# Three seams of a three-layer kernel: only TensorE keeps the written order, output blocks run in pairs, residual transfers move to SP's queue

## The chip, the cores and the metric

The kernel runs on one core of one Trainium2 chip. The metric is the device time of one execution in microseconds. Before the change the median of three runs is 1291.76 us (1290.72 to 1292.23). The engines are named as the profile names them: PE is TensorE, DVE is VectorE, ACT is ScalarE, POOL is GpSimd and SP is SyncE, which here only issues DMAs.

## The reference

Three layers run one after the other on 512 tokens of width 1024, in float32:

```python
for i in range(2):                       # first_block
    h = rms_norm(x, pre_norm[i])
    y = gla_mixer(h, ...) if i == 0 else nsa_mixer(h, ...)   # both end in  o @ w_out
    x = x + rms_norm(y, post_norm[i])
# second_block, one hybrid layer
h = rms_norm(x, norm_gain) * (1 + scale) + shift             # scale, shift, gate from c
proj = h @ w_in
attn = stick_breaking_attention(q, k, v)
p_a = (attn * silu(z_a)) @ w_branch_a
p_b = (multiscale_causal_pool(u) * silu(z_b)) @ w_branch_b
out = (sigmoid(m_a) * p_a + sigmoid(m_b) * p_b) @ w_out
return rms_norm(x + gate * out, final_gain)
```

What matters here are the three places where one layer ends and the next begins: an output product of 512x1024 by 1024x1024, a norm of its rows, the addition to the residual, a second norm, and then the first product of the next layer. The last of them ends the kernel.

## The kernel before

Every float32 product is made of three matmuls on rounded high and low parts (`w_hi` with `hH`, `w_lo` with `hH`, `w_hi` with `hL`). A weight comes in units of 256 columns (280 for `w_tok`). `load_unit` fetches a unit in two halves of 512 KB into `w_raw`, which has two buffers, over SP's queue (L146); ACT rounds each half to `w_hi` (L149), DVE subtracts to get `w_lo` (L150), and only then is the raw buffer free for the half that comes next. ORDER is a list of the units in the order in which they are fetched ahead.

A **seam** is the stretch around one output product. There are three: GLA's output into the NSA layer (about 205 to 325 us), NSA's output into the stick-breaking (SB) layer (about 625 to 750 us), and the last one (from about 1233 us to the end). In each, `out_products` works through eight blocks (b, n): b is one of four groups of 128 tokens, n is one half of the 1024 output columns. A block is 48 matmuls of 256 columns, 24 for each of its two weight units, so a block with n = 0 needs units 0 and 1, and a block with n = 1 needs units 2 and 3. PSUM tiles for even b have the name `ps_pj`, those for odd b `ps_sc`.

At the first two seams `boundary` follows a block up. `each` copies the product to `x` on ACT (L463) and sums its squares (L384). When both halves of a group b are there, the generator `norm` is put in a list of chains with a due step. It computes the root on DVE (`rms`, ten small operations), multiplies and adds the residual `xr` (L424, L425), sums squares again on ACT, stores the new residual stream to `x1d` or `x2d` by DMA, pauses 4 steps, computes `rms` and the scaled copy `xs` (L432), pauses 4 steps, and then lets PE transpose `xs` (L438), ACT scale the transposes into `ntmp` (L443 or L445) and round them to `hH` (L448), and DVE make `hL` (L449). The first products of the next layer read `hH` and `hL`: groups 0 and 1 first, then 2 and 3. A step is one `tick`, which `proj_toks` calls every 12 matmuls of an output block.

What sets the order: between `in_order` and its end, the order of PE, DVE, ACT and POOL is the order in which the program emits the instructions, so each engine works through that list and waits in it. The rounding of a weight half is not emitted at once there: it goes to a list `splits` with a due step (`late`, else `lag`), and `run_splits` emits one per tick. SP is not in that set; its instructions are put in order by a scheduler. The residual reads (`reload`) and the stores of the residual stream are issued from POOL. The pool `wout` holds units 2 and 3 of the output weight; at the third seam it also holds the 2 MB residual `x2`, which is one DMA on SP's queue ahead of the loads of units 2 and 3.

Of the kernel before, what the change touches and what calls it, by code (L numbers as in the profile page):

```python
# [75 lines left out]
def tile_kernel(ctx, tc, xT, xR, post_r0, post_r1, fgain_r, pos, vecs, w_gla, w_glr, w_gk, w_gla_out, w_nsa, w_tok, w_nsa_out, b_gate,  # L76
                pe_k, pe_v, ck1, cv1, ck2, cv2, cvec, w_ada, w_in2, pool_w, w_ba, w_bb, w_o2, out, dbg=None):
    nc = tc.nc
    V, S, G, TE = nc.vector, nc.scalar, nc.gpsimd, nc.tensor
# [6 lines left out]
    def f32(ap):  # L86
        return ap.bitcast(F32)
# [46 lines left out]
    splits = None  # L134
# [33 lines left out]
    def tick():  # L168

        nonlocal step  # L170
        step += 1
        for ch in chains[:]:
            while ch[0] <= step:
                d = next(ch[1], None)
                if d is None:
                    chains.remove(ch)
                    break
                ch[0] = step + d
        run_splits()

    @contextmanager
    def in_order():

        nonlocal splits
        E = mybir.EngineType
        with tc.manual_schedule(engines={E.PE, E.DVE, E.Activation, E.Pool}):
            splits = []
            yield
            while chains:
                tick()  # L190
            while splits:
                splits.pop(0)[2]()
        splits = None
# [34 lines left out]
    def psum(tag):  # L228
        return ps.tile([P, 512], F32, tag=tag, name="ps_" + tag, bufs=BANKS[tag])
# [47 lines left out]
    def proj_toks(jobs, aH, aL, need=None):  # L277

        for k in range(KC):
            if need:  # L280
                if k % max(1, 4 // len(jobs)) == 0:
                    tick()
                    ensure(*(u for u, _, _, _ in jobs))
                need(jobs[0][1] * P, k)
            for (wh, wl), tb, p, n in jobs:
                s = slice(tb * P, tb * P + P)
                TE.matmul(p[:, :n], aH[:, k, s], wh[:, k, :n], start=(k == 0), stop=False)  # L287
                TE.matmul(p[:, :n], aH[:, k, s], wl[:, k, :n], start=False, stop=False)  # L288
                TE.matmul(p[:, :n], aL[:, k, s], wh[:, k, :n], start=False, stop=(k == KC - 1))  # L289
# [81 lines left out]
    xt = x.rearrange("p c t -> p (c t)").rearrange("p (b d) -> p b d", b=NB)  # L371

    def half(n):
        return slice(n * 512, n * 512 + 512)

    def rms(ss):

        v = npl.tile([P, 1], F32, tag="rsv1", name="rsv", bufs=2)
        V.scalar_tensor_tensor(v, ss[:, 0:1], EPS, ss[:, 1:2], op0=ALU.add, op1=ALU.add)
        return rsqrt(v, 1)  # L380

    def square_sum(src, ss, n):
        scr = npl.tile([P, 512], F32, tag="scr", name="scr", bufs=1)
        S.activation(scr, src, AF.Square, scale=1.0 / 32, accum_out=ss[:, n:n + 1])  # L384
# [6 lines left out]

    def reload(src, b, n):
        r = npl.tile([P, 512], F32, tag="xr", name="xr", bufs=3)
        G.dma_start(r, src[:, b, half(n)])
        return r

    def split_x():
# [3 lines left out]

    def out_products(us, each, freed=lambda: None):

        for b, n in ((0, 0), (1, 0), (2, 0), (0, 1), (1, 1), (3, 0), (2, 1), (3, 1)):
            p = psum("sc" if b % 2 else "pj")
            for i in range(2):
                proj_toks([(us[2 * n + i], b, p[:, 256 * i:256 * i + 256], 256)], hH, hL, lambda t0, k: None)
            each(b, n, p)
            if (b, n) == (3, 0):
                freed()  # L410

    def boundary(wsrc, gain, xsrc, keep, scale, shift, then, early, fp):

        norms_, chunks = {}, [0] * NB

        def norm(b, ss, xo):
            y = rms(ss)  # L420
            ss2 = npl.tile([P, 2], F32, tag="ss2", name="ss2", bufs=2)
            for n in range(2):
                xn_ = xt[:, b, half(n)]
                V.scalar_tensor_tensor(xn_, xn_, y, grow[:, half(n)], op0=ALU.mult, op1=ALU.mult)  # L424
                V.tensor_add(xn_, xn_, xo[n])  # L425
                square_sum(xn_, ss2, n)
            G.dma_start(keep[:, b], xt[:, b])
            yield 4
            y = rms(ss2)
            xs = [npl.tile([P, 512], F32, tag="xs", name="xs", bufs=2) for n in range(2)]  # L430
            for n in range(2):
                S.activation(xs[n], xt[:, b, half(n)], AF.Copy, scale=y)  # L432
            yield 4
            ts = slice(b * P, b * P + P)
            for n in range(2):
                pt = psum("tr")
                for i in range(4):
                    TE.transpose(pt[:, i * P:(i + 1) * P], xs[n][:, i * P:(i + 1) * P], ident)  # L438
                tmp = npl.tile([P, 4, P], F32, tag="ntmp", name="ntmp", bufs=2)
                for i in range(4):  # L440
                    c = 4 * n + i
                    if shift is None:
                        S.activation(tmp[:, i], pt[:, i * P:(i + 1) * P], AF.Copy, scale=scale[:, c:c + 1])  # L443
                    else:
                        S.activation(tmp[:, i], pt[:, i * P:(i + 1) * P], AF.Identity, scale=scale[:, c:c + 1],  # L445
                                     bias=shift[:, c:c + 1])
                cs = slice(4 * n, 4 * n + 4)
                S.copy(hH[:, cs, ts], tmp)  # L448
                V.tensor_sub(hL[:, cs, ts], tmp, f32(hH[:, cs, ts]))  # L449
                chunks[b] += 4  # L450
                yield 1

        def need(t0, k):
            for b in (t0 // 256 * 2, t0 // 256 * 2 + 1):
                while chunks[b] <= k:
                    next(norms_[b][1])

        SS, nus = {}, []

        def each(b, n, p):  # L460
            if n == 0:
                SS[b] = npl.tile([P, 2], F32, tag="ss", name="ss", bufs=4)
            S.copy(xt[:, b, half(n)], p)  # L463
            square_sum(p, SS[b], n)
            if n:
                norms_[b] = [step + 2, norm(b, SS[b], [reload(xsrc, b, n_) for n_ in range(2)])]
                chains.append(norms_[b])
                if b == 2:
                    nus.append(unit(*then[0]))

        with tc.tile_pool(name="wout", bufs=2) as pool:
            us = [unit(wsrc, u) for u in range(2)]
            us += [load_unit(wsrc, u, pool=pool, late=4 * u - 3) for u in (2, 3)]
            grow = row_of(gain)
            firsts = [load_unit(*u, pool=fp, late=13 + 4 * i) for i, u in enumerate(early)]
            out_products(us, each, go_on)
            nus.append(unit(*then[1]))
        return nus, firsts, need
# [81 lines left out]
    with tc.tile_pool(name="gla", bufs=1) as gp:  # L560
# [24 lines left out]
        keep = gp.tile([P, 8, 64], F32, name="keep")  # L585
# [217 lines left out]
    prefetch(2)  # L803
    split_x()
    first = ExitStack()
    first.enter_context(in_order())
    o = VEC["pre1"][0]
    fps = ExitStack()
    uts, ucs, need = boundary(w_gla_out, post_r0, xR, x1d, vec[:, o:o + 8], None, ((w_tok, 0), (w_tok, 1)),
# [311 lines left out]
    nc.sync.dma_start(gated.rearrange("c p -> p c"), mod[:, 16:24])  # L1121
    prefetch(2)
    split_x()
    first.enter_context(in_order())
    uvs, (uq, uk), need = boundary(w_nsa_out, post_r1, x1d, x2d, amul, mod[:, 0:8], ((w_in2, 8), (w_in2, 9)),
                                   ((w_in2, 0), (w_in2, 4)),
                                   fps.enter_context(tc.tile_pool(name="sb_first", bufs=2, side="right")))
# [3 lines left out]
    with tc.tile_pool(name="sb_qk", bufs=1) as qp, tc.tile_pool(name="sb_v", bufs=2) as vp, ExitStack() as later:  # L1131
# [182 lines left out]
        while chains:  # L1314
            tick()
        norms.close()
        u_first = between.enter_context(tc.tile_pool(name="u_first", bufs=1, side="right"))
        gp = later.enter_context(tc.tile_pool(name="sb", bufs=1))

# [127 lines left out]
    lag = 5  # L1447
    prefetch(2)
    split_x()
    with in_order(), tc.tile_pool(name="wout", bufs=2) as pool:  # L1450
        us = [unit(w_o2, u) for u in range(2)] + [load_unit(w_o2, u, pool=pool, late=4 * u - 3) for u in (2, 3)]
        x2 = pool.tile([P, NB, D], F32, name="x2", bufs=1)
        nc.sync.dma_start(x2, x2d)
        gate, fgain = row_of(gated.rearrange("c p -> (c p)")), row_of(fgain_r, "fgain")
        SS = {}

        def last(b):
            y = rms(SS[b])
            for n in range(2):
                xn_ = xt[:, b, half(n)]  # L1460
                V.scalar_tensor_tensor(xn_, xn_, y, fgain[:, half(n)], op0=ALU.mult, op1=ALU.mult)
                nc.sync.dma_start(out[:, b, half(n)], xn_)
            yield 0

        def each(b, n, p):
            if n == 0:
                SS[b] = npl.tile([P, 2], F32, tag="ss", name="ss", bufs=4)
            xn_ = xt[:, b, half(n)]
            V.tensor_mul(xn_, p, gate[:, half(n)])
            V.tensor_add(xn_, xn_, x2[:, b, half(n)])  # L1470
            square_sum(xn_, SS[b], n)
            if n:
                chains.append([step + 1, last(b)])

        out_products(us, each)
# [85 lines left out]
```

## Time and profile before

| | us |
|---|---|
| median of the runs (lowest, highest) | 1291.76 (1290.72, 1292.23) |
| the profiled execution | 1293.02 |
| its span | 1291.3 |
| PE busy in it | 1204.9 (93%) |
| mean granted clock of PE, share of full speed | 0.972 |

The profiled execution took 1.3 us more than the median and 1.7 us more than its own span. A wait of PE in the lists below is the idle time of PE ahead of an instruction and names the instruction of another engine that ended it. The granted clock is given as a share of 2.4 GHz; the chip's records of this kernel have two levels, 1.2 and 2.4 GHz, so a mean clock c over a stretch of L us says that 2(1-c)L us of it were at 1.2 GHz.

### The profile page before, as it was taken

How to read it: one execution, taken by the hardware profiler on the slowest of the kernel's cores; microseconds unless marked ns; L12 is line 12 of the kernel's file. 1: busy time of each engine (PE TensorE's matmuls, PEld its weight loads, DVE VectorE, ACT ScalarE, POOL GpSimd, SP SyncE). 2: the span in 40 equal slices, each digit the busy share in tenths (PEclk: the TensorE clock that was granted, in tenths of full speed). 3: DMA queues.
4: the chain of work that ended last, by engine and by line, in shares of the span. 5: the costliest groups of instructions: out<-in, count | busy, mean ns of one | idle time of the engine just before them, and what ended most of it. 6: DMA issues, size and time to landing. Idle time of an engine off the chain costs nothing.

```text
span 1291.3 us, 18606 instructions
## 1 busy us (share of the span) xinstructions
PE 1204.9 (93%) x6880; PEld 1021.9 (79%) x6880; DVE 809.6 (63%) x1534; ACT 627.4 (49%) x1308; POOL 292.2 (23%) x422
## 2 busy tenths in 40 slices
PE   6998999879989999999986999999999999999996
PEld 6788778879867777777886977889887878888886
DVE  7668886562569888776556258778857552223445
ACT  6542136551537767678555456766644332222321
POOL 2113121010002433323001046555613410000000
PEclk9999999889989999999988989999999999999998
DMA  6244734432442011111443022212124233322241
GB/s 200 66 163 160 237 90 155 139 119 84 140 125 60 13 50 33 46 37 33 131 131 115 1 66 66 65 56 77 65 75 146 74 98 98 95 88 93 93 155 66
DMA packets 38843, 122.76 MB, mean 95 GB/s; under 512 B 6352, under 2 KB 8528, under 8 KB 38112
## 3 DMA queue, kind: packets, MB, share of 16 engines
q1 hardware_dynamic: 36320, 113.18, 27.6%
q0 software_dynamic: 2432, 8.39, 2.0%
q8 instruction: 54, 0.88, 0.3%
q14 instruction: 37, 0.30, 0.1%
HBM read 111.58 MB, written 6.30 MB: 91 GB/s over the span
## 4 chain that ended last, share of the span: by engine, by line
PE 59%; DVE 16%; ACT 11%; issue 6%; DMA 4%; POOL 4%; SPq 0%; ACTq 0%; DVEq 0%; POOLq 0%
PE ps_pj L236 6%; PE ps_pj L238 6%; PE ps_pj L237 6%; ACT w_hi L149 3%; DVE w_lo L150 3%; PE ps_tr L491 3%; PE ps_pv L1083 3%; PE ps_sc L237 3%; PE ps_sc L236 3%; PE ps_sc L238 3%; PE ps_pj L247 2%; PE ps_pj L245 2%; PE ps_pj L246 2%; POOL us L1377 2%; PE ps_sc L288 1%
## 5 line engine op out<-in xcount | busy, mean ns | idle before, releaser
L150 DVE TENSOR_TENSOR w_lo<-w_raw,w_hi 128x1024 fp32r<-128x1024 f32 (+1 forms) x154 | 190.4, 1247 | 132.2 <-ACT w_hi L149 127.6
L149 ACT CAST w_hi<-w_raw 128x1024 fp32r<-128x1024 f32 (+1 forms) x154 | 159.0, 1050 | 161.1 <-PE ps_sc L237 60.1
L236 PE MATMUL ps_pj<-hH,w_hi 128*128 128x512 f32 x512 | 207.3, 405 | 8.7 <-DVE rtm L844 4.6
L238 PE MATMUL ps_pj<-hH,w_lo 128*128 128x512 f32 x512 | 206.9, 404 | 0.0
L237 PE MATMUL ps_pj<-hL,w_hi 128*128 128x512 f32 x512 | 205.9, 402 | 0.0
L236 PEld LDWEIGHTS ps_pj<-hH,w_hi 128*128 128x128 f32 x512 | 97.3, 190 | 33.2 <-issue 6.7
L1071 POOL TENSOR_SCALAR PB<-PB,sm 128x128 f32<-128x128 f32 (+3 forms) x128 | 76.8, 622 | 181.8 <-DVE sm L1067 112.5
L238 PEld LDWEIGHTS ps_pj<-hH,w_lo 128*128 128x128 f32 x512 | 97.3, 190 | 20.7 <-issue 0.5
L237 PEld LDWEIGHTS ps_pj<-hL,w_hi 128*128 128x128 f32 x512 | 97.1, 190 | 19.8 <-issue 0.2
L495 ACT CAST PTh<-ps_tr 128x512 fp32r<-128x512 f32 (+3 forms) x160 | 74.3, 481 | 68.7 <-PE ps_tr L491 64.5
L496 DVE TENSOR_TENSOR PTl<-ps_tr,PTh 128x512 fp32r<-128x512 f32 (+3 forms) x160 | 85.7, 550 | 33.6 <-ACT PTh L495 32.3
L287 PE MATMUL ps_pj<-w_hi,hH 128*128 128x256 f32 (+1 forms) x288 | 85.9, 299 | 14.1 <-ACT w_hi L577 8.3
L287 PE MATMUL ps_sc<-w_hi,hH 128*128 128x256 f32 (+1 forms) x320 | 92.9, 291 | 1.8 <-ACT w_hi L149 1.8
L288 PE MATMUL ps_sc<-w_lo,hH 128*128 128x256 f32 (+1 forms) x320 | 92.3, 289 | 0.6 <-DVE w_lo L150 0.6
L289 PE MATMUL ps_sc<-w_hi,hL 128*128 128x256 f32 (+1 forms) x320 | 91.8, 288 | 0.0
L289 PE MATMUL ps_pj<-w_hi,hL 128*128 128x256 f32 (+1 forms) x288 | 84.4, 294 | 4.3 <-DVE hL L357 4.3
L288 PE MATMUL ps_pj<-w_lo,hH 128*128 128x256 f32 (+1 forms) x288 | 84.7, 294 | 1.1 <-POOL w_lo L578 0.7
L245 PE MATMUL ps_pj<-hH,w_hi 128*128 128x512 f32 x176 | 72.7, 413 | 3.0 <-ACT w_hi L149 3.0
L1064 ACT ACTIVATE PB<-ps_sc,nmx 128x128 f32<-128x128 f32 (+3 forms) x128 | 66.7, 534 | 14.6 <-DVE nmx L1061 7.1
L247 PE MATMUL ps_pj<-hH,w_lo 128*128 128x512 f32 x176 | 70.8, 402 | 0.1
L246 PE MATMUL ps_pj<-hL,w_hi 128*128 128x512 f32 x176 | 70.7, 402 | 0.0
L287 PEld LDWEIGHTS ps_pj<-w_hi,hH 128*128 128x128 f32 x288 | 56.9, 198 | 15.0 <-ACT w_hi L577 8.3
(365 smaller groups left out, 2935.3 us busy)
## 6 DMA issues: line engine op xcount, KB each, us to landing
w_raw<-in_w_in_dram SPq DMA_DIRECT2D x64, 512.0 KB, 3.3
wada<-in_w_ada_dram SPq DMA_DIRECT2D x24, 512.0 KB, 4.3
w_raw<-in_w_nsa_dram SPq DMA_DIRECT2D x24, 512.0 KB, 3.7
w_raw<-in_w_gla_dram SPq DMA_DIRECT2D x22, 512.0 KB, 4.4
w_raw<-in_w_gla_out_dram SPq DMA_DIRECT2D x8, 512.0 KB, 4.1
w_raw<-in_w_nsa_out_dram SPq DMA_DIRECT2D x8, 512.0 KB, 3.3
w_raw<-in_w_bb_dram SPq DMA_DIRECT2D x8, 512.0 KB, 3.6
w_raw<-in_w_ba_dram SPq DMA_DIRECT2D x8, 512.0 KB, 4.2
```

What stands on the lines that cost most here:

```text
L149: S.copy(hi[:, :, s], raw)
L150: lo_on[j].tensor_sub(lo[:, :, s], raw, f32(hi[:, :, s]))
L236: TE.matmul(p[:m, :tn], wh[:, k, s], aH[:, k, ts], start=(k == 0), stop=False)
L237: TE.matmul(p[:m, :tn], wh[:, k, s], aL[:, k, ts], start=False, stop=False)
L238: TE.matmul(p[:m, :tn], wl[:, k, s], aH[:, k, ts], start=False, stop=(k == KC - 1))
L245: TE.matmul(p, wh[:, k, s], aH[:, k], start=(k == 0), stop=False)
L246: TE.matmul(p, wh[:, k, s], aL[:, k], start=False, stop=False)
L247: TE.matmul(p, wl[:, k, s], aH[:, k], start=False, stop=(k == KC - 1))
L287: TE.matmul(p[:, :n], aH[:, k, s], wh[:, k, :n], start=(k == 0), stop=False)
L288: TE.matmul(p[:, :n], aH[:, k, s], wl[:, k, :n], start=False, stop=False)
L289: TE.matmul(p[:, :n], aL[:, k, s], wh[:, k, :n], start=False, stop=(k == KC - 1))
L496: V.tensor_sub(pl[:, :m], pt[:, :m], f32(ph[:, :m]))
```

## The change

Five things change, at the seams only.

1. `in_order(True)` keeps the written order for PE alone. `splits` is then None, so the rounding of a weight half is emitted where the load is, and the scheduler puts ACT, DVE, POOL and SP in order by its own estimate. It holds through the SB layer's first products too, where a `first.close()` and a new `in_order()` bring the old regime back.
2. The blocks run in the order (0,0) (1,0) (0,1) (1,1) (2,0) (3,0) (2,1) (3,1) instead of (0,0) (1,0) (2,0) (0,1) (1,1) (3,0) (2,1) (3,1). `out_products` serves all three seams.
3. The two pauses in `norm` are 5 steps instead of 4.
4. `reload` and the stores of `x1d` and `x2d` are issued from SP instead of POOL: 8 reads of 256 KB and 4 writes of 512 KB at each of the first two seams.
5. The pool `wout` of `boundary` is opened with `reuse_waits="tile"`; that of the third seam is not.

```diff
-    def in_order():
+    def in_order(alone=False):
...
-        with tc.manual_schedule(engines={E.PE, E.DVE, E.Activation, E.Pool}):
-            splits = []
+        with tc.manual_schedule(engines={E.PE} if alone else {E.PE, E.DVE, E.Activation, E.Pool}):
+            splits = None if alone else []
...
-        G.dma_start(r, src[:, b, half(n)])
+        nc.sync.dma_start(r, src[:, b, half(n)])
...
-        for b, n in ((0, 0), (1, 0), (2, 0), (0, 1), (1, 1), (3, 0), (2, 1), (3, 1)):
+        for b, n in ((0, 0), (1, 0), (0, 1), (1, 1), (2, 0), (3, 0), (2, 1), (3, 1)):
...
-            G.dma_start(keep[:, b], xt[:, b])
-            yield 4
+            nc.sync.dma_start(keep[:, b], xt[:, b])
+            yield 5
...
-            yield 4
+            yield 5
...
-        with tc.tile_pool(name="wout", bufs=2) as pool:
+        with tc.tile_pool(name="wout", bufs=2, reuse_waits="tile") as pool:
...
-    first.enter_context(in_order())          # first and second seam
+    first.enter_context(in_order(True))
...
+        first.close()                        # after the SB layer's first products
+        first.enter_context(in_order())
...
-    with in_order(), tc.tile_pool(name="wout", bufs=2) as pool:      # third seam
+    with in_order(True), tc.tile_pool(name="wout", bufs=2) as pool:
```

On ACT at the first seam, before: in the written order the squares of group 2 (`scr` from `x`) and a rounding of `w_tok` stand between the two `hH` of group 1.

```order
L443 ACTIVATE ntmp<-ps_tr,vec 128x128 x4
L448 CAST hH<-ntmp 128x4x128
L384 ACTIVATE scr,ss_2566<-x 128x512 x2
L149 CAST w_hi<-w_raw 128x8x140
L443 ACTIVATE ntmp<-ps_tr,vec 128x128 x4
L448 CAST hH<-ntmp 128x4x128
```

The same place on ACT now.

```order
L443 ACTIVATE ntmp<-ps_tr,vec 128x128 x4
L149 CAST w_hi<-w_raw 128x8x140
L448 CAST hH<-ntmp 128x4x128
L463 COPY x<-ps_pj 128x512
L384 ACTIVATE scr,ss<-ps_pj 128x512
L443 ACTIVATE ntmp<-ps_tr,vec 128x128 x4
L448 CAST hH<-ntmp 128x4x128
```

The squares taken from `x`, which wait for DVE's chain of the other group, have left the place between the two `hH`; a copy of a product block and its squares stand there instead.

On SP at the second seam, before: the loads of the output weight and of the gain row, then the weights of the next layer, with nothing between.

```order
L146 DMA w_raw<-in_w_nsa_out_dram 128x1024 x5
L389 DMA grow<-in_post_r_dram 128x1024
L146 DMA w_raw<-in_w_nsa_out_dram 128x1024 x3
L146 DMA w_raw<-in_w_in_dram 128x1024 x39
```

The same place on SP now; `xr` are the residual reads, `x2d` the stores.

```order
L389 DMA grow<-in_post_r_dram 128x1024
L146 DMA w_raw<-in_w_nsa_out_dram 128x1024
L394 DMA xr<-x1d 128x512 x2
L146 DMA w_raw<-in_w_nsa_out_dram 128x1024
L394 DMA xr<-x1d 128x512
L146 DMA w_raw<-in_w_nsa_out_dram 128x1024
L146 DMA w_raw<-in_w_in_dram 128x1024 x5
L394 DMA xr<-x1d 128x512
L146 DMA w_raw<-in_w_in_dram 128x1024
L427 DMA x2d<-x 128x1024
L394 DMA xr<-x1d 128x512 x2
```

The residual reads of group 0 now stand ahead of the two halves of unit 3, and the second read of group 1 behind five halves of the next layer's weights.

On ACT where the SB layer's first products end, before: the rounding of the next unit (`w_hi`) comes behind a table load and two activations of the first attention slot.

```order
L1148 CAST SV<-ps_sc 128x4x64 x2
L1245 ACT_TABLE_LOAD
L1245 ACTIVATE be<-ps_sc 128x256
L1246 ACTIVATE sg<-ps_sc 128x256
L149 CAST w_hi<-w_raw 128x8x128 x2
```

The same place now.

```order
L149 CAST w_hi<-w_raw 128x8x128 x2
L1148 CAST SV<-ps_sc 128x4x64 x2
L1245 ACT_TABLE_LOAD
L1245 ACTIVATE be<-ps_sc 128x256
L1246 ACTIVATE sg<-ps_sc 128x256
```

The two roundings have moved ahead of the last copies of `SV`.

## Rows read from the trace of the kernel before

**Rows 1.** The page, its span and part 1 (busy, share, instructions).

```profile
span 1291.3 us, 18606 instructions
...
PE 1204.9 (93%) x6880; PEld 1021.9 (79%) x6880; DVE 809.6 (63%) x1534; ACT 627.4 (49%) x1308; POOL 292.2 (23%) x422
```

**Rows 2.** Waits of PE, 200 to 340 us: total, times, longest.

```profile
PE ps_tr L438 <- ACT xs L432: 7.5, 3, 3.1
PE ps_pj L273 <- ACT hH L448: 5.3, 1, 5.3
...
PE ps_pj L236 <- ACT w_hi L149: 1.6, 2, 1.4
```

**Rows 3.** Waits of PE, 620 to 800 us.

```profile
PE ps_tr L438 <- ACT xs L432: 8.8, 3, 4.5
PE ps_pj L273 <- ACT hH L448: 5.5, 1, 5.5
PE ps_pj L245 <- ACT w_hi L149: 3.0, 1, 3.0
PE ps_pj L287 <- DVE SQs L1170: 2.7, 2, 1.6
```

**Rows 4.** Stretches: length, busy of PE, PEld, DVE, ACT, POOL, clock, DMA, GB/s.

```profile
200.00:340.00 140.00, 122.01 (x929) 117.91 (x928) 73.45 (x168) 69.27 (x144) 11.25 (x21) 0.95 0.42 134
620.00:760.00 140.00, 118.39 (x854) 113.69 (x855) 67.93 (x161) 72.83 (x155) 14.31 (x29) 0.89 0.30 98
...
1240.00:1244.00 4.00, 4.00 (x36) 4.00 (x35) 0.71 (x2) 0.00 (x0) 0.00 (x0) 1.00 0.97 401
```

**Rows 5.** ACT's timeline, first seam: start, duration, instruction, idle before it.

```profile
222.70 0.59 ACT L463 COPY x<-ps_pj 128x512 f32<-128x512 f32 x1 [0.36 <-PE ps_pj L289]
...
228.39 0.59 ACT L463 COPY x<-ps_pj 128x512 f32<-128x512 f32 x1 [0.32 <-PE ps_pj L289]
...
236.07 0.64 ACT L384 ACTIVATE scr<-x 128x512 f32<-128x512 f32 x1 [4.72 <-DVE x L425]
...
242.27 1.33 ACT L432 ACTIVATE xs<-x,rsy 128x512 f32<-128x512 f32 x2 [2.08 <-DVE rsy L307]
```

**Rows 6.** DVE's timeline in the same stretch.

```profile
231.38 1.23 DVE L150 TENSOR_TENSOR w_lo<-w_raw,w_hi 128x1024 fp32r<-128x1024 f32 x1 [2.05 <-ACT w_hi L149]
232.52 0.15 DVE L379 SCALAR_TENSOR_TENSOR rsv<-ss 128x1 f32<-128x1 f32 x1
...
234.49 0.75 DVE L424 SCALAR_TENSOR_TENSOR x<-x,rsy,grow 128x512 f32<-128x512 f32 x1
```

**Rows 7.** ACT's timeline ahead of the longest wait of that seam.

```profile
264.11 0.63 ACT L384 ACTIVATE scr<-x 128x512 f32<-128x512 f32 x1 [4.13 <-DVE x L425]
...
266.18 1.11 ACT L149 CAST w_hi<-w_raw 128x1120 fp32r<-128x1120 f32 x1
267.20 1.13 ACT L443 ACTIVATE ntmp<-ps_tr,vec 128x128 f32<-128x128 f32 x4
```

**Rows 8.** ACT's timeline where the SB layer's first products end.

```profile
746.18 1.28 ACT L1245 ACT_TABLE_LOAD   x1
...
748.01 1.99 ACT L149 CAST w_hi<-w_raw 128x1024 fp32r<-128x1024 f32 x2
```

**Rows 9.** ACT's timeline, second seam: last half of unit 3, then the third block.

```profile
639.35 1.05 ACT L149 CAST w_hi<-w_raw 128x1024 fp32r<-128x1024 f32 x1 [1.52 <-DMA w_raw<-in_w_nsa_out_dram]
641.41 0.59 ACT L463 COPY x<-ps_pj 128x512 f32<-128x512 f32 x1 [1.01 <-PE ps_pj L289]
```

**Rows 10.** PE's timeline, third seam, middle of block (0,1).

```profile
1255.66 0.39 PE L288 MATMUL ps_pj<-w_lo,hH 128*128 128x256 f32 x1 [0.38 <-DVE w_lo L150]
```

**Rows 11.** DMA issues, 624 to 660 us: count, KB each, median us to landing.

```profile
w_raw<-in_w_nsa_out_dram SPq DMA_DIRECT2D x4, 512.0 KB, 3.6
xr<-x1d POOLq DMA_DIRECT2D x4, 256.0 KB, 5.7
```

**Rows 12.** What SP's queue waited for, 200 to 340 us.

```profile
SPq L146 <- DVE w_lo L150: 43.9, 14, 8.4
```

More of the change, by code (lines that the diff above doesn't have):

```diff
@@ L1123, in tile_kernel @@
     split_x()
-    first.enter_context(in_order())
+    first.enter_context(in_order(True))
     uvs, (uq, uk), need = boundary(w_nsa_out, post_r1, x1d, x2d, amul, mod[:, 0:8], ((w_in2, 8), (w_in2, 9)),
```

## The prediction

> **What bounds the kernel now.** I read the page first: PE is busy 1204.9 of 1291.3 us [rows 1], so nothing but idle PE or a slow PE can be won back, 86 us in all. Then the list of PE's waits, cut to the first two seams. At the first, PE waits 7.5 us in three pieces for the scaled copies `xs` of the norm, 5.3 us in one piece for `hH` and 1.6 us for a rounded weight: 14.4 us [rows 2]. At the second it waits 8.8 and 5.5 us for the same two, 3.0 us for a weight that ACT rounds late and 2.7 us for `SQs`: 20.0 us [rows 3]. Then the table of stretches: over 140 us around each seam the mean granted clock is 0.95 and 0.89 [rows 4], so 2 x 0.05 x 140 = 14 us and 2 x 0.11 x 140 = 31 us ran at 1.2 GHz instead of 2.4. Those stretches follow the waits; PE loses half of them, less the part in which it is idle anyway. Last, the timelines of ACT and DVE, to see why the norm is late.
>
> There, group 0 of the first seam is the pattern. Its last block is copied at 228.39 us; blocks are 228.39 - 222.70 = 5.69 us apart, which is 48 matmuls at 0.119 us [rows 5]. The copy and its squares need about 1.3 us, so the norm could begin near 229.7. DVE begins it at 232.52, right behind a weight split of 1.23 us that was emitted ahead of it [rows 6]. The two squares of the residual stream follow at 236.07, after ACT had idled 4.72 us, and the `xs` start at 242.27; the first is ready after half of 1.33 us [rows 5], 14.6 us after the copy began. About 3 us of the 14.6 are the late start; the chain itself takes 11 to 12. The longest wait has another cause: ACT stands 4.13 us at the squares of a later group, whose input DVE has not made, then rounds a half of `w_tok` for 1.11 us, and only then scales the transposes of group 1, at 267.20 [rows 7]. PE needed them before that.
>
> **The change, part by part.** *Blocks in pairs, longer pauses.* In PE's written order 108 matmuls stood between the end of group 0's last block and its transposes, 12.8 us. Now (1,1), (2,0) and 36 matmuls of (3,0) stand there, 132 or 15.6 us, which covers the 14.6 even if nothing in the chain becomes faster. I count 132 to 140 matmuls for the other groups too. Between the second half of group 1's transposes and the first product that reads them stand 48 matmuls or 5.7 us, where there were 24 or 2.9.
>
> *Order on ACT, DVE and POOL.* The squares that blocked ACT for 4.13 us no longer stand between the two `hH` of group 1. The scheduler puts what it expects to be ready first, so a wrong expectation can cost what the written order cost; a rounding of `w_tok` still stands there, 1.11 us. I leave 3.5 of the first seam's 14.4 us (bounds 0 and 14.4): the last two groups have little between their transposes and their first use, 12 to 36 matmuls or 1.4 to 4.3 us, beside about 1.13 us for four scaled copies and as much again for `hH` and `hL`. That is **-10.9**. Where the SB layer's first products end, the table load of 1.28 us and two activations held the next unit's roundings until 748.01 [rows 8]; these now stand ahead, so the wait of 3.0 goes. Of the second seam's 20.0 us I leave 5 (bounds 0 and 20), more than at the first because a residual read now stands behind five weight halves there: **-15.0**.
>
> *Weights one block earlier.* Block (0,1) is the first to need units 2 and 3, and it moves from fourth to third place: 5.7 us earlier, while nothing in the third seam makes its loads earlier. The order of SP and ACT is the same there and its `wout` pool is untouched. Before, the second half of (0,1) started when DVE's last `w_lo` of unit 3 was done, at 1255.66, with a wait of 0.38 [rows 10]: already on the edge. Now the same matmul starts at the same time by the clock of the loads, but with one whole block fewer done. The loss is that block: **+5.7** (bounds 3, if the scheduler's freedom on DVE pulls a split forward, and 6.5). Two waits of about 2 and 4 us bring a low clock with them: **+2.0** (0 to 4). At the second seam the last rounding of unit 3 starts at 639.35 and takes 1.05 us, its split 1.23 us [rows 6, 9], so it was done at 641.6. The third block is copied at 641.41, so (0,1) started there [rows 9]; now it starts at 635.7 and its second half wants unit 3 at 638.6. With unchanged loads PE waits 3.0 us. Up to 1.7 more come if the three residual reads now ahead of it in SP's queue cost their own transfer time; nothing if the first halves, rounded when they land and not at a due step, free `w_raw` 3 us sooner. I take **+2.0** (0 to 4.7). At the first seam the loads of unit 3 were early enough to move by a block, and I take 0.
>
> *The DMA queue.* POOL's 12 issues per seam go and SP gains them; both engines wait most of the time, so issuing costs nothing. A residual read of 256 KB took 5.7 us from POOL beside weight halves of 512 KB that took 3.6 from SP [rows 11]. On SP's queue reads and weights follow one another. Over the third seam's 2 MB load that queue alone moved 401 GB/s [rows 4], far above the 134 and 98 GB/s of the seams, so its rate does not bind; what can bind is its order. The Trainium skill, "DMA: Bandwidth & Descriptors", section "Issuing engines are not separate DMA queues", says that DMAs run on the same 16 engines and interleave whichever engine issues them, so a second issuer adds no bandwidth; the 401 GB/s from one queue agree. By that rule the move costs no bandwidth, and the sum would be the same.
>
> *Clock.* Of the 45 us at 1.2 GHz, PE was idle in part of them. If all 34.4 us of waits lay inside, (45 - 34.4) / 2 = 5 us are lost; if none, 22. Waits come before the low stretch and reach into it, so I take 16 us lost now. With 10.5 of 34.4 us of waits left, a third of it stays: **-11.0** (0 to -20).
>
> *Sum.* -10.9 - 15.0 + 5.7 + 2.0 + 2.0 - 11.0 = -27.2. The profiled execution took 1293.0 us, so 1265.8; the median of the runs lies 1.3 us below it, which gives **1264.5 us**, and I predict 1265. Its own range is 1256 to 1274.
>
> **The rivals.** *Half of the gain.* The waits shrink but do not go, and a short wait still brings a low clock: 17 us of waits stay instead of 10.5, the clock gives back 5 instead of 11: 6.5 + 6 us more, 1277.5. For it: the scheduler's order is an estimate, and 1.6 us of rounding waits lie in the first seam already. Against it: the extra 24 matmuls per group need no estimate.
>
> *All of it.* No wait of the norms is left, unit 3 is in time at the second seam, the clock stays up: 8.5 + 2 + 5 us less, 1249. For it: cover above the chain for all groups. Against it: the third seam's loss is in all cases.
>
> *Slower: one queue, one order.* SP issues in order and each weight half waits for a free raw buffer, up to 8.4 us at a time at this seam, 43.9 us in all [rows 12]. A residual read behind five such halves (at 3.6 us each, if they do not overlap, 18 us) reaches a norm that wants it within 2 to 3 us of its block, and a store that waits for a norm holds the weights behind it. If reads come more than the 1.0 us of slack (15.6 - 14.6) late for each group, the waits stay as long as they were, 34.4 us and their clock; the third seam's 7.7 and the second's 2.0 remain: 1291.8 + 9.7 = 1301. It decides from about 4 us of lateness per group, eight groups. Against it: halves overlap, with two buffers and a queue that was idle for much of the seam.
>
> *No net change.* The waits of the norms fall by no more than the new waits for weights and their clock bring, about 10 us: 1292.
>
> **How the numbers follow.** The forecast 0.48, half of the gain 0.23, all of it 0.13, slower 0.11, no net change 0.05. The range 1249 to 1289 takes in the first three and leaves out the last two and the far end of the third. This kernel's runs tell a change of about 0.2% or 2.6 us. Faster than that: 0.84; within it: 0.05; slower: 0.11.
>
> **What would show it.** In the profile after: the waits on `xs` and `hH` at both seams under 4 us each in total, and the mean clock of the two 140 us stretches above 0.96. The wait of 3.0 us on a rounded weight at the SB layer's start gone. A new pair of waits at the third seam on `w_hi` and `w_lo` of units 2 and 3, 5 to 7 us together, with the same landing times counted from the seam's start. At the second seam a wait of 0 to 5 us in front of (0,1). I am wrong if the `xs` waits stay because their residual read lands late (then SP's order decides), or if the third seam shows no new wait.

## The result and the profile after

The changed kernel takes 1245.73 us (median of 4 runs, 1245.01 to 1249.45) against 1291.99 for the kernel before (4 runs): a ratio of 0.9649, 95% interval 0.9628 to 0.967, or 46.3 us less. The forecast was 1265 with a range down to 1249; the time lies 3 us below the range, near the rival "all of it" (1249). The profiled execution took 1246.3 us, its span is 1244.6 us, its mean granted clock 0.989 where it was 0.972.

The page, span and part 1, against [rows 1]:

```profile
span 1244.6 us, 18577 instructions
...
PE 1188.1 (95%) x6880; PEld 1010.8 (81%) x6880; DVE 800.6 (64%) x1534; ACT 626.8 (50%) x1308; POOL 279.1 (22%) x398
```

PE's busy time fell by 16.8 us with the same 6880 matmuls: that is work done at the higher clock. The other 30 us of the 46.7 are idle time that went.

All waits of PE between 200 and 335 us (engine, line, what it waited for; total, times, longest), against [rows 2]:

```profile
PE ps_pj L289 <- DVE hL L357: 2.4, 1, 2.4
```

The three waits of before, 14.4 us together, are gone, and nothing took their place: the row that is left is a wait in the first output block, which was 2.4 us before too.

The waits of PE between 590 and 760 us that belong to the seam, against [rows 3]:

```profile
PE ps_tr L438 <- ACT xs L432: 2.1, 1, 2.1
...
PE ps_pj L288 <- DVE w_lo L150: 0.9, 1, 0.9
PE ps_pj L287 <- ACT hH L356: 0.8, 1, 0.8
PE ps_tr L438 <- ACT ntmp L445: 0.6, 1, 0.6
```

Of 20.0 us, 2.1 are left; 0.6 on `ntmp` and 0.9 in the middle of block (0,1) came new. The wait of 3.0 us for a weight at the SB layer's start and that on `SQs` are gone.

The stretches around the first two seams and the start of the third, columns as in [rows 4]:

```profile
200.00:340.00 140.00, 137.49 (x1091) 131.84 (x1090) 78.17 (x190) 74.55 (x165) 6.71 (x12) 0.99 0.44 145
595.00:735.00 140.00, 133.87 (x978) 125.95 (x976) 82.24 (x185) 89.61 (x186) 24.58 (x38) 0.99 0.33 110
1180.00:1210.00 30.00, 24.47 (x170) 23.44 (x169) 13.40 (x19) 8.76 (x14) 0.00 (x0) 0.89 0.39 141
```

The clock of 0.95 and 0.89 became 0.99 and 0.99: of 45 us at 1.2 GHz some 6 are left. In the third seam 2 x 0.11 x 30 = 6.6 us at 1.2 GHz came new.

PE's timeline in the middle of block (0,1) of the third seam, against [rows 10]:

```profile
1201.58 0.38 PE L287 MATMUL ps_pj<-w_hi,hH 128*128 128x256 f32 x1 [0.85 <-ACT w_hi L149]
1202.84 0.39 PE L288 MATMUL ps_pj<-w_lo,hH 128*128 128x256 f32 x1 [0.88 <-DVE w_lo L150]
```

Counted from the seam's first wait on `hL` (1237.68 before, 1184.50 after), the matmul that needs unit 3's `w_lo` starts at 17.98 before and at 18.34 now. It waits for the same thing at nearly the same time, with one block fewer done.

Where the time went, by spans of the two traces. The marks are the starts of the first matmul after each seam's wait on `hL` L357, of the first L940 and of the first L1289 on `PTl`.

| stretch | before | after | difference |
|---|---|---|---|
| up to the first seam | 207.0 | 203.6 | -3.4 |
| first seam and NSA's first products | 122.4 | 102.0 | -20.4 |
| NSA layer | 297.4 | 295.8 | -1.6 |
| second seam and SB's first products | 150.0 | 123.4 | -26.6 |
| SB and pool branch | 461.0 | 459.7 | -1.3 |
| third seam to the end | 53.6 | 60.1 | +6.5 |

The first, third and fifth rows are stretches that the change leaves alone. Over the 15 profiles (the two kernels and the 13 versions below) the first takes 203.6 to 208.4 us, the third 295.8 to 297.9, the fifth 459.5 to 461.1. Stretches at 1.2 GHz come and go there in the same code; of the 6.3 us that the three rows add here, 5.7 are busy time of PE. In the eleven versions made from the changed kernel the three add up to 961.4 to 966.4 us, against 965.4 before and 959.1 here, so the 6.3 us are not counted to the change. The seams alone give 40.5 us.

### The profile page after: what moved, and what is told of

It is laid out like the page before. It is cut to its first block, busy times and chain, and to the rows that moved or that the text cites. A ratio compares the mean times of both kernels' runs of the same rounds, so it can differ in the third digit from the quotient of the medians.

```text
span 1244.6 us, 18577 instructions
## 1 busy us (share of the span) xinstructions
PE 1188.1 (95%) x6880; PEld 1010.8 (81%) x6880; DVE 800.6 (64%) x1534; ACT 626.8 (50%) x1308; POOL 279.1 (22%) x398
## 4 chain that ended last, share of the span: by engine, by line
PE 63%; DVE 13%; ACT 8%; issue 6%; DMA 5%; POOL 4%; SPq 0%; DVEq 0%; ACTq 0%; POOLq 0%
PE ps_pj L236 6%; PE ps_pj L238 6%; PE ps_pj L237 5%; DVE w_lo L150 3%; PE ps_tr L491 3%; PE ps_pv L1083 3%; PE ps_sc L237 3%; PE ps_sc L236 3%; PE ps_sc L238 3%; ACT w_hi L149 3%; PE ps_sc L288 2%; PE ps_sc L289 2%; PE ps_sc L287 2%; PE ps_pj L245 2%; PE ps_pj L247 2%
## 5 line engine op out<-in xcount | busy, mean ns | idle before, releaser
L149 ACT CAST w_hi<-w_raw 128x1024 fp32r<-128x1024 f32 (+1 forms) x154 | 159.0, 1052 | 169.4 <-PE ps_sc L237 60.4
L238 PEld LDWEIGHTS ps_pj<-hH,w_lo 128*128 128x128 f32 x512 | 96.6, 189 | 20.4 <-issue 0.2
L237 PEld LDWEIGHTS ps_pj<-hL,w_hi 128*128 128x128 f32 x512 | 96.7, 189 | 19.5 <-issue 0.2
L1064 ACT ACTIVATE PB<-ps_sc,nmx 128x128 f32<-128x128 f32 (+3 forms) x128 | 66.7, 534 | 14.4 <-DVE nmx L1061 7.1
```

The source lines that it names most:

```text
L149: S.copy(hi[:, :, s], raw)
L237: TE.matmul(p[:m, :tn], wh[:, k, s], aL[:, k, ts], start=False, stop=False)
L238: TE.matmul(p[:m, :tn], wl[:, k, s], aH[:, k, ts], start=False, stop=(k == KC - 1))
```

## The experiments

Times are medians, with the ratio to the kernel before and its interval. "Seams" gives the second, fourth and last rows of the table above for that kernel's profile.

**Old blocks in the third seam.**

```diff
-        out_products(us, each)
+        out_products(us, each, old=True)     # (0,0) (1,0) (2,0) (0,1) ... there alone
```

> The changed kernel, but the third seam alone works through its eight blocks in the old order. My theory: pairs cost the third seam one block, 5.7 us, and about 1 us of low clock, because units 2 and 3 cannot come earlier there; the trace shows the third seam 6.5 us longer than before. Then this runs at 1239 to 1240 us, the waits on w_hi and w_lo of that seam fall from 4.2 us to under 1 us. Rival: the third seam is longer because ACT and DVE are ordered by the scheduler there; then this stays at 1245 to 1246.

Measured 1242.79 us, 0.9623 (0.9605 to 0.9642); seams 101.9, 123.2, 52.1. The only wait over 0.2 us that is left in its third seam:

```profile
PE ps_pj L289 <- DVE hL L357: 1.4, 1, 1.4
```

The seam is 8.0 us shorter than with pairs, though the scheduler orders ACT and DVE there as well; the rival falls. The median gained 3 us, not the 6 expected, and its interval overlaps that of the changed kernel: its profile spent 2.4 and 2.0 us more ahead of the first seam and in the NSA layer, in code that is the same.

**Written order back at the first two seams.**

```diff
-    first.enter_context(in_order(True))
+    first.enter_context(in_order())
```

> The changed kernel with the written order of PE, DVE, ACT and POOL back at the first two seams (splits deferred again); pairs, pauses of 5, SP's queue and the third seam as changed. Theory A (the free order of ACT and DVE brings most, since late rounding and squares in front of the transposes held the norm): 1270 to 1280, waits on xs and hH back above 12 us. Theory B (the 24 more matmuls of cover bring most): 1248 to 1256, waits under 6 us, and the 3 us wait for a rounded weight at the SB layer's start back with its low clock.

Measured 1308.91 us, 1.0132 (1.0112 to 1.0151): slower than the kernel before; seams 132.6, 153.4, 60.4. Theory A was right on the cause and too mild by some 30 us. ACT's timeline shows why the longer pauses and the written order don't go together (start, duration, instruction, idle before it):

```profile
226.44 0.59 ACT L463 COPY x<-ps_pj 128x512 f32<-128x512 f32 x1 [6.62 <-PE ps_pj L289]
...
237.35 1.04 ACT L149 CAST w_hi<-w_raw 128x1024 fp32r<-128x1024 f32 x1
243.12 0.63 ACT L384 ACTIVATE scr<-x 128x512 f32<-128x512 f32 x1 [4.72 <-DVE x L425]
...
245.14 1.03 ACT L149 CAST w_hi<-w_raw 128x1024 fp32r<-128x1024 f32 x1
249.31 1.33 ACT L432 ACTIVATE xs<-x,rsy 128x512 f32<-128x512 f32 x2 [3.15 <-DVE rsy L307]
```

In both block orders groups 0 and 1 end 48 matmuls apart, which is 4 steps. With pauses of 4, group 0's `xs` came due in the same step as the first half of group 1's norm and stood ahead of it: in the kernel before, the `xs` at 242.27 [rows 5] come first and group 1's squares after them.

```profile
245.70 0.63 ACT L384 ACTIVATE scr<-x 128x512 f32<-128x512 f32 x1 [2.10 <-DVE x L425]
```

With pauses of 5 the whole first half of group 1's norm is emitted ahead of group 0's `xs`: ACT stands 4.72 us at group 1's squares at 243.12 before it may scale group 0. From the copy of group 0's last block at 226.44 to its first `xs` it takes 23.5 us. PE's waits between 200 and 335 us:

```profile
PE ps_tr L438 <- ACT xs L432: 18.1, 2, 10.5
PE ps_pj L287 <- ACT w_hi L149: 3.2, 1, 3.2
```

**POOL's queue back.**

```diff
-        nc.sync.dma_start(r, src[:, b, half(n)])
+        G.dma_start(r, src[:, b, half(n)])        # and the store of x1d, x2d
```

> The changed kernel with the residual reads and stores issued from POOL again. Theory A (rate is shared and the queue does not bind): within 2 us of 1245.7. Theory B (reads in SP's order keep the weights of units 2 and 3 in front and in time): 1249 to 1256, with a wait of 2 to 5 us in front of block (0,1) at the second seam. Theory C (reads in SP's order come late behind the weights): faster, 1242 to 1244, with the 2.1 us wait on xs at 660 us gone.

Measured 1246.38 us, 0.9658 (0.9635 to 0.968); seams 101.7, 123.4, 60.7. No difference can be told. Small waits changed places at the second seam: 2.1 us on `xs` are gone, but 1.5 on a rounded weight came new in the middle of (0,1), beside the 0.9 that was there:

```profile
PE ps_pj L287 <- ACT w_hi L149: 1.5, 1, 1.5
PE ps_pj L288 <- DVE w_lo L150: 1.1, 2, 0.9
```

With SP's order the last half of unit 3 is rounded 10.8 us after the seam's mark, with POOL's 12.7 us, in one profile each: the weights come earlier, as theory B had it, but the time is not in its range. The wait on `xs` is gone, as theory C had it, but not for its reason: in the changed kernel no addition of the residual (L425) in that seam finds DVE idle ahead of it, so the reads are in time. DVE's timeline ahead of that wait shows the last step of group 2's root (L307) behind 2.6 us of group 3's work:

```profile
657.25 1.40 DVE L424 SCALAR_TENSOR_TENSOR x<-x,rsy,grow 128x512 f32<-128x512 f32 x2
658.58 1.28 DVE L425 TENSOR_TENSOR x<-x,xr 128x512 f32<-128x512 f32 x2
659.78 0.14 DVE L307 SCALAR_TENSOR_TENSOR rsy<-rst,rsy 128x1 f32<-128x1 f32 x1
```

That is the scheduler's order on DVE, and with the reads on POOL it came out otherwise.

**Old blocks and pauses of 4 at the first two seams.**

```diff
-            out_products(us, each, go_on)
+            out_products(us, each, go_on, old=True)
-            yield 5
+            yield 4
```

> The changed kernel with the old block order and pauses of 4 at the first two seams; free order of ACT and DVE, SP's queue and the third seam as changed. Theory A (the free order brings most): 1248 to 1256, waits on xs and hH under 6 us in the two seams. Theory B (cover in PE's order brings most): 1265 to 1280, waits on xs and hH above 12 us.

Measured 1249.55 us, 0.9676 (0.9656 to 0.9696); seams 103.8, 121.5, 58.3. Theory A: pairs and pauses are worth at most some 4 us here, and by the spans of the first two seams nothing (225.3 us against 225.4).

**Pairs and pauses alone, on the kernel before.**

```diff
-        for b, n in ((0, 0), (1, 0), (2, 0), (0, 1), ...
+        for b, n in ((0, 0), (1, 0), (0, 1), (1, 1), ...   # first two seams; yield 4 -> yield 5
```

> The kernel before with two of the five parts alone: pairs and pauses of 5 at the first two seams; written order of all engines, POOL's queue, third seam as before. My theory now: with the written order the pairs bring the loads of units 2 and 3 into the way and the longer pauses make PE wait for xs; it is slower than before, 1297 to 1303, with waits on xs over 25 us. Rival: SP's queue, not the pairs, made the written order slow; then this runs at 1275 to 1290.

Measured 1304.9 us, 1.0093 (1.0078 to 1.0108); seams 131.4, 154.8, 52.8. It is slower, as expected, by 1.9 us more than the range given, with waits on `xs` of 18.4 us at the first seam; POOL's queue is the old one, so SP's is not the reason. Pairs and pauses were not run apart: the rows above put the waits on `xs` down to the pauses, and no run tells what pairs alone cost in the written order.

**The free order alone, on the kernel before.**

```diff
-    first.enter_context(in_order())
+    first.enter_context(in_order(True))       # splits = None with it, closed after SB's first products
```

> The kernel before with one part alone: at the first two seams only PE keeps the written order and roundings are emitted at the load; old block order, pauses of 4, POOL's queue, no tile waits, third seam as before. My theory: this part alone brings nearly all of it, and as the third seam keeps its old blocks it is faster than the whole change: 1240 to 1244, waits on xs and hH under 6 us in the two seams. Rival: it needs SP's queue or the pairs beside it; then 1252 to 1275.

Measured 1249.17 us, 0.9658 (0.9643 to 0.9672); seams 105.4, 124.2, 52.5. One part of five brings 43.7 of the 46.3 us. By the spans of the three seams it gains even more than the whole change, 43.9 us against 40.5, as its third seam keeps the old blocks. The 1240 to 1244 expected was missed: waits of 1.9 us on `hH` at the first seam and of 2.0, 1.4 and 0.9 at the second stayed.

**Free order, roundings late again.**

```diff
-            splits = None if alone else []
+            splits = None if alone and not late_splits else []
```

> The changed kernel, but at the first two seams the roundings are again emitted late, by due step; the order of ACT, DVE and POOL stays the scheduler's. If the scheduler's order is what counts, 1244 to 1252. If emitting the roundings at the load is what counts, 1270 to 1309, with waits on xs and on w_hi.

Measured 1244.82 us, 0.9631 (0.9612 to 0.9651); seams 100.6, 119.0, 59.8. Emitting the roundings at the load is not what counts. The second seam is 4.4 us shorter than in the changed kernel, in one profile each.

**Written order, roundings at the load.**

```diff
-            splits = None if alone else []
+            splits = None if alone or now else []      # all four engines in written order
```

> The changed kernel, but at the first two seams all four engines keep the written order, with the roundings emitted at the load, not by due step. If the scheduler's order is what counts, it stays slow, 1280 to 1310, since ACT then waits for each load in its place. If the early rounding is what counts, 1244 to 1260.

Measured 1294.74 us, 1.0016 (0.9999 to 1.0034); seams 123.6, 146.9, 59.7. Against the written order with late roundings (1308.91) the early rounding gives 14 us, and in the free order it gives nothing. With this and the one above, the two halves of the first part are apart: the order that the scheduler gives is the gain.

**ACT alone in the written order, and DVE alone.**

```diff
-    first.enter_context(in_order(True))
+    first.enter_context(in_order(True, lambda E: {E.PE, E.Activation}))   # {E.PE, E.DVE} in the second version
```

> The changed kernel, but at the first two seams ACT keeps the written order beside PE (DVE, POOL and SP free). If ACT's order is the one that held the norm (squares of another group in front of the scaled transposes, as before at 264 us), 1280 to 1300; if DVE's is, 1245 to 1256.

> The changed kernel, but at the first two seams DVE keeps the written order beside PE (ACT, POOL and SP free). If ACT's order is the one that counts, 1245 to 1256; if DVE's (the whole chain of one group's norm emitted in one piece ahead of the subtraction that makes hL for another), 1275 to 1300.

ACT written: 1281.26 us, 0.9924 (0.9894 to 0.9954); seams 118.8, 140.1, 58.6. DVE written: 1273.59 us, 0.9868 (0.9837 to 0.9898); seams 115.1, 135.3, 60.7. Neither forecast named one engine rightly: either order alone gives back 28 to 36 us (the second lies 1.4 us under its range). PE's waits between 200 and 335 us, ACT written and then DVE written:

```profile
PE ps_tr L438 <- ACT xs L432: 7.4, 2, 4.7
...
PE ps_pj L236 <- ACT w_hi L149: 1.6, 2, 1.4
PE ps_pj L287 <- ACT scr L384: 1.4, 1, 1.4
```

```profile
PE ps_tr L438 <- ACT xs L432: 9.9, 2, 6.5
```

The norm passes between the two engines four times up to `xs`, so one of them in a fixed list holds the other. These lists are the ones with pauses of 5, where the first half of group 1's norm stands ahead of group 0's `xs`; ACT's timeline with ACT written shows it again:

```profile
241.96 0.63 ACT L384 ACTIVATE scr<-x 128x512 f32<-128x512 f32 x1 [4.09 <-DVE x L425]
...
243.34 1.32 ACT L432 ACTIVATE xs<-x,rsy 128x512 f32<-128x512 f32 x2
```

What one engine's list would cost with pauses of 4 was not run.

**x2 by token groups in the third seam.**

```diff
-        x2 = pool.tile([P, NB, D], F32, name="x2", bufs=1)
-        nc.sync.dma_start(x2, x2d)
...
+                x2[b] = pool.tile([P, D], F32, tag="x2", name="x2", bufs=2)
+                nc.sync.dma_start(x2[b], x2d[:, b])
```

> The changed kernel; in the third seam the residual x2 is not one load of 2 MB ahead of units 2 and 3 but one load of 512 KB per token group, two buffers, so only 512 KB to 1 MB stand ahead of the weights. My theory: the third seam's waits are the load chain of units 2 and 3 behind the 2 MB; they shrink from 4.2 us of waits and the seam from 60 us to 53 to 56 us counted from its first wait to the end; the run takes 1239 to 1243. Rival: the chain through the two raw buffers (load, round, subtract, load) binds whatever stands ahead; then the seam stays within 1.5 us.

Measured 1241.3 us, 0.9615 (0.9587 to 0.9643); seams 100.7, 123.1, 54.0. The seam is 6.1 us shorter with pairs kept, and the run lies in the range of the theory: the loss is the load chain behind the 2 MB.

**Both mends of the third seam.** The two edits together:

> A version meant to beat both: the changed kernel with the old block order in the third seam and x2 loaded by token groups there. If the two mend the same loss, 1238 to 1243, like the better of the two alone; the seam from its first wait to the end takes 52 us, with no wait on a rounded weight over 0.5 us.

Measured 1242.9 us, 0.9607 (0.9566 to 0.9648); seams 101.1, 123.3, 51.6. They mend the same loss and do not add.

**The best version:** both mends and the late roundings.

> The changed kernel with the roundings emitted late at the first two seams (order still the scheduler's), the old block order in the third seam and x2 loaded by token groups. My theory: both gains add, as they lie in different seams; from the profiles 4 us at the second seam, 1 at the first, 8 at the third: 1232 to 1238, with no wait on xs or hH over 0.5 us and no stretch at 1.2 GHz between 205 and 350 us and between 595 and 720 us. Rival: what differs between such versions is the low clock outside the seams, which comes and goes in the same code; then 1240 to 1244.

Measured 1236.9 us (6 runs, 1233.48 to 1244.11), 0.9575 (0.9546 to 0.9605): below the changed kernel's interval, and 55.6 us under the kernel before; seams 100.6, 118.5, 51.7. These are all of PE's waits between 590 and 720 us:

```profile
PE ps_pj L287 <- ACT hH L356: 0.8, 1, 0.8
PE ps_pj L288 <- DVE w_lo L150: 0.8, 1, 0.8
PE ps_pj L289 <- DVE hL L357: 0.5, 1, 0.5
```

Its stretches around the three seams:

```profile
200.00:340.00 140.00, 136.38 (x1100) 130.81 (x1099) 79.41 (x191) 75.40 (x166) 6.48 (x12) 1.00 0.45 147
595.00:735.00 140.00, 134.39 (x988) 126.15 (x987) 86.16 (x191) 94.11 (x195) 27.35 (x44) 1.00 0.33 110
1180.00:1210.00 30.00, 28.65 (x241) 28.44 (x240) 14.01 (x18) 7.38 (x14) 0.00 (x0) 1.00 0.38 123
```

With no wait of the norms left, nothing in these stretches runs at 1.2 GHz, though the waits of 0.5 to 0.8 us above and one of 2.4 us on `hL` at the first seam stay. The gains of different seams add: the spans of the three seams are 14.7 us shorter than in the changed kernel, where late roundings alone gave 6.1 and both mends alone 9.5. The median gained 8.8.

The part `reuse_waits="tile"` alone was not run. The free order alone reaches 43.7 of 46.3 us without it.

## Why the prediction was wrong

**The direction and the places were right.** The waits on `xs` and `hH` went, the 3.0 us at SB's start went, the third seam lost a block, and block (0,1) of the second seam waits 0.9 us where 0 to 4.7 were given. One reading was short from the start: the 86 us are PE's idle time alone, and what a slow PE loses lies in its busy time and comes on top.

The profiled sum fell short by 19.5 us (-27.2 against -46.7). These are the three seams from mark to mark, columns as in [rows 4], the kernel before first:

```profile
206.97:329.32 122.35, 106.77 (x806) 103.79 (x806) 60.47 (x152) 55.18 (x118) 9.94 (x18) 0.94 0.38 122
626.76:776.72 149.96, 129.25 (x893) 121.82 (x894) 72.10 (x161) 79.07 (x163) 22.25 (x38) 0.90 0.30 97
1237.68:1291.32 53.64, 43.37 (x361) 42.96 (x361) 28.31 (x69) 9.88 (x20) 0.00 (x0) 0.94 0.30 112
```

```profile
203.56:305.60 102.04, 102.04 (x809) 101.03 (x810) 56.72 (x151) 55.00 (x117) 4.79 (x8) 0.98 0.45 144
601.36:724.77 123.41, 119.16 (x893) 113.71 (x894) 68.19 (x161) 78.67 (x163) 16.38 (x26) 0.99 0.35 118
1184.50:1244.59 60.09, 47.16 (x361) 46.17 (x361) 28.19 (x69) 9.76 (x20) 0.00 (x0) 0.91 0.26 98
```

**The failed step is what was left standing.** The terms "I leave 3.5" and "I leave 5" of the norms' waits and "+2.0" at (0,1) kept 10.5 us; the trace after shows 0 at the first seam and 2.1 + 0.6 + 0.9 = 3.6 at the second. They were guesses at how badly a scheduler's estimate would do, with no row behind them. By PE's idle time in the first two seams, which holds short gaps too, 23.9 us were forecast to go and 32.0 went, from 36.3 to 4.3. That is 8.1 of the 19.5 us.

**The clock term failed with it.** PE's busy time in the two seams fell from 236.0 to 221.2 us with the same work, 14.8 us, where "a third of it stays" gave 11.0 of the 16 lost. That is 3.8 us. The 16 were about right, as 14.8 went with some of the low clock still there; what failed is the third that stays. By the mean clocks 45 us ran at 1.2 GHz before and some 6 after, a stretch of 3.4 us in each seam, which is a seventh.

The rest of the 19.5 are 1.2 us at the third seam and the 6.3 us outside the seams, which are not counted to the change. Without these 6.3 the time would be 1252 us, inside the stated range: that it lies below is in part luck.

**The reason given for the gain was wrong.** The forecast said that 132 matmuls of cover suffice "even if nothing in the chain becomes faster". The experiments show the opposite. Pairs and pauses in the written order made the chain 23.5 us long, longer than the cover of 15.6, and the time went up to 1304.9 and 1308.91. The chain is not a fixed 14.6 us; the order on ACT and DVE decides it. The free order shortens it, by the timelines of the changed kernel, against [rows 5] and [rows 6]:

```profile
220.72 0.59 ACT L463 COPY x<-ps_pj 128x512 f32<-128x512 f32 x1
...
221.93 0.16 DVE L379 SCALAR_TENSOR_TENSOR rsv<-ss 128x1 f32<-128x1 f32 x1
...
226.43 0.64 ACT L384 ACTIVATE scr<-x 128x512 f32<-128x512 f32 x1
...
232.37 1.34 ACT L432 ACTIVATE xs<-x,rsy 128x512 f32<-128x512 f32 x2 [2.10 <-DVE rsy L307]
```

From the copy to the first `xs` it is now 12.3 us. DVE begins the norm 1.2 us after the copy begins, where it was 4.1 before: the late start of about 3 us that the prediction had read is gone, and from DVE's first step to the first `xs` it takes 11.1 us, 10.4 before. With the free order, the old blocks and pauses of 4 the same stretch takes 9.4 us, under the 12.8 us of cover that the old blocks give, and PE has no wait on `xs` at that seam:

```profile
228.76 0.58 ACT L463 COPY x<-ps_pj 128x512 f32<-128x512 f32 x1
...
237.50 1.34 ACT L432 ACTIVATE xs<-x,rsy 128x512 f32<-128x512 f32 x2 [0.90 <-DVE rsy L307]
```

So the extra cover was not needed there, which fits the at most 4 us that this version lost.

**The third seam** was forecast at +5.7 and +2.0 and came to +6.5. Its waits grew from 0.4 to 4.2 us. By the windows above PE's idle time there grew by 2.6 us and its busy time, part of it at 1.2 GHz, by 3.8; both mends, of the order and of the load, show that the cause was the one given.

**The queue** cost nothing, as forecast. The rival of one queue and one order did not show: no residual read came late at the second seam, and the 2.1 us on `xs` there are the scheduler's order on DVE, which the prediction had named as a danger ("a wrong expectation can cost what the written order cost").

**What stays open** is why the low clock in the untouched stretches comes and goes. The runs of the changed kernel spread over 4.4 us and those of the best version over 10.6, with a mean granted clock of 0.993 in its fastest and 0.987 in its slowest run; gains of that size are hidden in a few runs.

## What to carry to other kernels

Where a chain passes from engine to engine several times, a fixed order on any one of them can set the length of the chain, and here more cover on the engine that waits did not help: look at what stands ahead of the chain's next instruction in its own queue. Where a list is written by due steps, a pause longer than the distance between two chains puts the start of the second ahead of the end of the first. An order of work that suits two places can cost at a third where the loads are not early enough; compare when the data are ready with when they are now wanted, by place. Price the low clock with the waits ahead of it: here the waits went from 36 to 4 us of idle time and the low clock from 45 to some 6.

## What the runs showed of the hardware

The same code at the same place took 203.6 to 208.4 us in 15 profiles, up to the first seam. The two ends of that range differ in their stretches at 1.2 GHz: beside one of 3.4 us near 22 us in both, the changed kernel has one of 3.4 us near 97.5, the version with x2 by groups 6.8 us near 98 and 3.4 us more near 135.5. PE's busy time there is 183.3 us in the one and 186.2 in the other, so 2.9 of the 4.9 us are busy time and the rest is idle time.
